# Mixers B and C of a hybrid diffusion block: zero-padded products replaced by pairs of 64-row products

## The chip, the cores and the metric

The kernel runs on one core of one Trainium2 chip. The metric is the device time of one execution in microseconds (us). A change of under 0.2% cannot be told from none on this kernel.

## The reference

One layer of a backbone over 2048 latent tokens of 1024 channels, with 256 context tokens that share its weights. After a norm and one input projection three groups of heads work side by side: A, a gated linear recurrence; B, gated linear attention (6 heads of 64); C, an mLSTM matrix memory (6 heads of 64). All run in both directions. Their outputs are normalised and gated, go through an output projection and then a squared-ReLU MLP. The change lies in the chunked products of B and C (chunks of 64 in the reference, of 128 in the kernel, which is the same sum):

```
B:  scores  = where(causal, q_dec @ k_dec.T, 0)         # per head, direction and chunk
    out     = scores @ v  +  q_dec @ s_prev
C:  w       = (q @ k.T) * exp(log_d - m_row)            # per head; q @ k.T serves both directions
    num     = w @ v  +  e_in * (q @ C_prev)             # second term: the carried product
    C_prev  is updated per chunk by  e_end * k.T @ v
```

Each q @ k.T and q @ C_prev contracts over the 64 channels of one head.

## The kernel before

The program is one in-order list for TensorE (PE): its instructions stand as the code emits them. The other engines' lists are ordered by a scheduler that keeps data dependences. The input projection is cut into small pieces, three matmuls each (lines 365 to 367), and a filler (`fil.run(us)`) drops so many us of them between the products of the mixers, so that PE has work while other engines prepare the next operand.

**Mixer C** (`mix_c`, from line 805) walks 16 chunks of 128 tokens, three pairs of heads each: 48 steps. Two heads lie on the two halves of the partitions. Step i puts on PE, in this order: `scores(i+1)` (line 898: one product of `k3` with `q6`, whose other half is zero for each head, 128 contraction rows, 256 columns); for the first pair of a chunk transposes of the keys (830), for the second the state update `upd_s` (841, weights 64 columns wide); filler; `outputs(i)` (925: four products of 65 columns); `carried(i+1)` (913: two products of 130 columns with the zero-padded `q6`); filler. On VectorE (DVE) line 902 makes the decay weights, 905 multiplies them with the scores, 926 adds the output products to the carried term, 847 updates the state. ScalarE (ACT) takes the exponential (904) and copies the carried product out of PSUM (916).

PSUM has 8 banks: 3 for `pp`, 1 for `tr`, and in mixer C 2 for `qk` (two buffers), 1 for `o2` (carried products and state updates), 1 for `o1` (output products).

**Mixer B's output part** (end of `mix_b`) walks 24 steps (4 groups of 512 tokens, 6 heads). `scores(i+2)` loads q and k (both directions of a head on the two halves of the partitions), copies the two halves of q into a zero-padded tile `bx` (1147 on ACT, 1148 on DVE), makes four products of 256 columns (1155), and takes them from PSUM by an ACT copy and a DVE predicated copy in two halves (1157, 1158), then 1159. `between(i)` follows with filler or pieces of the output projection (1264 to 1266), then `outputs(i)` (1166, 1167). The q tile has 4 buffers, the k tile 3, and the loads are issued in order by SyncE (SP).

An fp32 product stands in the trace as two passes, each a weight load (PEld) and a MATMUL: 8 for the four products at line 1155.

Of the kernel before, what the change touches and what calls it, by code (L numbers as in the profile page):

```python
# [11 lines left out]
F32 = mybir.dt.float32  # L12
# [3 lines left out]
ALU = mybir.AluOpType  # L16
# [4 lines left out]
P = 128  # L21
# [90 lines left out]
def body(ctx: ExitStack, tc: tile.TileContext, I, out, dbg=None, stage=99):  # L112
    nc = tc.nc
# [24 lines left out]
    def spool(stack, name, side="right", bufs=1):  # L138
        return stack.enter_context(tc.tile_pool(name=name, bufs=bufs, side=side, reuse_waits="tile"))

    def psum(stack, name):
        return stack.enter_context(tc.tile_pool(name=name, bufs=1, space=PSUM, reuse_waits="tile"))
# [123 lines left out]
    for k in range(KC):  # L266
        for j in range(4):
            i = 4 * k + j
# [128 lines left out]
    def dgrp(nm, shape_of, groups, dt=F32):  # L397
        return {g: dram.tile(shape_of(GRP[g][1]), dt, name=f"{nm}_{g}") for g in groups}
# [67 lines left out]
    qcD = dgrp("qcD", lambda n: [3, P, n], LATG)  # L466
# [339 lines left out]
    def mix_c():  # L806
        st = ExitStack()
        cp = spool(st, "mxc")
        pm = psum(st, "pmc")

        qz = [cp.tile([P, 6, P], F32, name=f"qz{i}") for i in range(2)]
        for t_ in qz:
            nc.gpsimd.memset(t_, 0.0)
        csD = [dram.tile([P, 3, 65], F32, name=f"csD{c}") for c in range(NCH)]

        def load_kv(c):
            g = 0 if c < 2 else 1 + (c - 2) // 4
            o = c * P - GRP[g][0]
            k3 = cp.tile([P, 3, P], F32, name="k3", bufs=2)
            nc.sync.dma_start(k3, kcD[g][:, :, o:o + P].rearrange("b p t -> p b t"))  # L820
            v3 = cp.tile([P, 6, 65], F32, name="v3", bufs=2)
            nc.gpsimd.memset(v3[:, :, 64:65], 1.0)
            nc.sync.dma_start(v3[:, :, 0:64], vcD[g][o:o + P, :].rearrange("t (h e) -> t h e", e=64))
            return g, o, k3, v3
# [10 lines left out]

        def upd_s(c, d, kb, v3, s_old, s_new):

            u = pm.tile([P, 512], F32, name="o2", bufs=1)
            for h in range(6):
                p, hl = h // 2, h % 2  # L840
                nc.tensor.matmul(u[64 * hl:64 * hl + 64, p * 65:p * 65 + 65], kb[:, h, :], v3[:, h, :])
            for p in range(3):
                up = u[:, p * 65:p * 65 + 65]
                if s_old is None:
                    nc.vector.tensor_copy(s_new[:, p, :], up)
                else:
                    nc.vector.scalar_tensor_tensor(s_new[:, p, :], s_old[:, p, :], abc[:, p, d, c:c + 1], up,
                                                   op0=ALU.mult, op1=ALU.add)
# [4 lines left out]
        for c in [1, 0] + list(range(NCH - 1, 2, -1)) + [None]:  # L853
            if c is not None:
                g, o, k3, v3 = load_kv(c)
# [14 lines left out]
        for c in range(2):  # L870
            g, o, k3, v3 = load_kv(c)
# [8 lines left out]

        def head(c):
            g, o, k3, v3 = load_kv(c)
            q6 = qz[c % 2]
            for hl in range(2):
                hs = slice(64 * hl, 64 * hl + 64)
                nc.sync.dma_start(q6[hs, hl::2, :], qcD[g][:, hs, o:o + P].rearrange("b p t -> p b t"))
            ys = cp.tile([P, 3, P], F32, name="yc", bufs=2)
            cur[c] = (g, o, k3, v3, q6, ys)

        def scores(c, p):  # L890
            if p == 0:
                head(c)
            g, o, k3, v3, q6, ys = cur[c]
            rb = cp.tile([P, 2, 2, P], F32, name="rb", bufs=2)
            for d in range(2):
                nc.sync.dma_start(rb[:, :, d, :], rD[d][g][2 * p:2 * p + 2, o:o + P].unsqueeze(0).to_broadcast([P, 2, P]))
            qk = pm.tile([P, 512], F32, name="qk", bufs=2)
            nc.tensor.matmul(qk[:, 0:256], k3[:, p, :], q6[:, 2 * p:2 * p + 2, :])
            w = cp.tile([P, 2, 2, P], F32, name="wd", bufs=2)
            for hl in range(2):  # L900
                for d in range(2):
                    nc.vector.scalar_tensor_tensor(w[:, hl, d, :], rb[:, hl, d, :], TM[:, c, 0, 2 * p + hl, d:d + 1],
                                                   lm[:, d, :], op0=ALU.add, op1=ALU.min)
            nc.scalar.activation(w, w, AF.Exp)
            nc.vector.tensor_tensor(w, w, qk[:, 0:256].rearrange("p (h l) -> p h l", h=2).unsqueeze(2).to_broadcast([P, 2, 2, P]),
                                    op=ALU.mult)
            return w

        def carried(c, p, states):
            q6 = cur[c][4]  # L910
            o2 = pm.tile([P, 512], F32, name="o2", bufs=1)
            for hl in range(2):
                nc.tensor.matmul(o2[:, hl * 130:hl * 130 + 130], q6[:, 2 * p + hl, :], states[:, p, :, :])
            nm = cp.tile([P, 4, 65], F32, name="nm", bufs=2)
            hd = TM[:, c, :, 2 * p:2 * p + 2, :].rearrange("p q h d -> p q (h d)")
            nc.scalar.copy(nm, o2[:, 0:260].rearrange("p (h e) -> p h e", e=65))
            nc.gpsimd.tensor_tensor(nm, nm, hd[:, 1, :].unsqueeze(2).to_broadcast([P, 4, 65]), op=ALU.mult)
            return nm, hd

        def outputs(c, p, w, nm, hd):  # L920
            g, o, k3, v3, q6, ys = cur[c]
            o1 = pm.tile([P, 512], F32, name="o1", bufs=1)
            for hl in range(2):
                for d in range(2):
                    nc.tensor.matmul(o1[:, (hl * 2 + d) * 65:(hl * 2 + d) * 65 + 65], w[:, hl, d, :], v3[:, 2 * p + hl, :])
            nc.vector.tensor_tensor(nm, nm, o1[:, 0:260].rearrange("p (h e) -> p h e", e=65), op=ALU.add)
            dn = cp.tile([P, 4], F32, name="dn", bufs=2)
            nc.vector.scalar_tensor_tensor(dn, nm[:, :, 64], -1.0, nm[:, :, 64], op0=ALU.mult, op1=ALU.max)
            nc.vector.tensor_tensor(dn, dn, hd[:, 3, :], op=ALU.max)
            nc.vector.reciprocal(dn, dn)  # L930
            yy = cp.tile([P, 4, 64], F32, name="yy", bufs=2)
            nc.gpsimd.tensor_tensor(yy, nm[:, :, 0:64], dn.unsqueeze(2).to_broadcast([P, 4, 64]), op=ALU.mult)
            y4 = yy.rearrange("p (h d) e -> p h d e", d=2)
            nc.gpsimd.tensor_tensor(ys[:, p, :].rearrange("p (h e) -> p h e", h=2), y4[:, :, 0, :], y4[:, :, 1, :], op=ALU.add)
            if p == 2:
                nc.sync.dma_start(yD[g][o:o + P, 640:1024], ys.rearrange("p a b -> p (a b)"))
                cur.pop(c)

        seq = [(c, p) for c in range(2, NCH) for p in range(3)]
        states = {2: s_fw}  # L940
# [5 lines left out]
        for i, (c, p) in enumerate(seq):  # L946
# [11 lines left out]
            w = ws.pop(i)  # L958
# [20 lines left out]
    def mix_b(between):  # L979
# [19 lines left out]
        pm = psum(st, "pmb")  # L999
        bp = spool(st, "mxb")  # L1000
# [4 lines left out]
        sel = bp.tile([P, P], I32, name="sel")  # L1005
# [103 lines left out]
        for i in range(LAST):  # L1109
            if i < len(seq):  # L1110
                hh, g = seq[i]
# [9 lines left out]
            if 0 <= i3:  # L1121
                hh, g = seq[i3]
# [8 lines left out]
            pass  # L1131

        qz = [bp.tile([P, 2, 512], F32, name="bx", bufs=3) for _ in range(3)]
        for t_ in qz:
            nc.gpsimd.memset(t_, 0.0)

        def scores(i, p, g, hl):
            hh = 2 * p + hl  # L1140
            q, k = bt("bk", 4), bt("bq", 3)
            nc.sync.dma_start(q, qdD[hh][g])
            nc.sync.dma_start(k, kdD[hh][g])
            s = bp.tile([P, 4, 64], F32, name="bv", bufs=3)
            nc.gpsimd.dma_start(s, sD[hh][:, 4 * g - 4:4 * g, :])
            z = qz[i % 3]
            nc.scalar.copy(z[0:64, 0, :], q[0:64, :])
            nc.vector.tensor_copy(z[64:128, 1, :], q[64:128, :])
            w = bt("lr" if i % 2 else "bkt")
            wv = w.rearrange("p (c l) -> p c l", l=P)  # L1150
            for jj in (0, 2):
                sc = pm.tile([P, 2, 2, P], F32, name="qk2", bufs=4)
                for j in range(2):
                    js = slice((jj + j) * P, (jj + j + 1) * P)
                    nc.tensor.matmul(sc[:, j, :, :], k[:, js], z[:, :, js])
                wj = wv[:, jj:jj + 2, :]
                nc.scalar.copy(wj, sc[:, :, 0, :])
                nc.vector.copy_predicated(wj, sel.unsqueeze(1).to_broadcast([P, 2, P]), sc[:, :, 1, :])
            nc.vector.tensor_tensor(wv, wv, eye1.unsqueeze(1).to_broadcast([P, 4, P]), op=ALU.mult)
            return q, s, w  # L1160

# [9 lines left out]
        o = v = None  # L1171
        for i in range(-2, len(seq)):
# [5 lines left out]
            p, g, hl = seq[i]  # L1178
            if hl == 0:
# [3 lines left out]
                o = trt()  # L1183
# [561 lines left out]
```

## Time and profile before

| what | value |
|---|---|
| time, median of 3 runs | 2805.06 us (2803.17 to 2809.77) |
| the profiled execution | 2810.26 us, of which its span is 2808.5 us |
| mean granted clock of TensorE | 0.958 |
| PE busy, DVE busy, ACT busy | 2559.5, 1775.4, 1162.4 us |
| mixer C's 48 steps | about 577 to 803 us of the span |
| mixer B's output part | about 1116 to 1281 us of the span |

PE is busy in 91% of the span. A busy row is modelled from the start of the MATMUL to its end, and MATMULs overlap in the pipeline, so the distance between starts tells the pace, not the duration of one.

### The profile page before, as it was taken

To read this page: it belongs to the slowest core of one execution; us is meant where nothing else is said; L and a number is where in the kernel's file an instruction comes from. 1 tells how busy PE (TensorE), PEld (TensorE's weight loads), DVE (VectorE), ACT (ScalarE), POOL (GpSimd) and SP (SyncE) were. 2 spreads that over 40 slices of the span, in tenths; PEclk is the share of its full clock that TensorE was granted. 3 is DMA by queue.
4 is the path that set the end of the run, shared out by engine and by line. 5 is a ranking of instruction groups with operands and counts; after the bars stand their busy time and mean duration, and the time that the engine had idled before them with its cause. 6 is when DMAs were issued, how large, how long until landed. Compare 5 with 4: busy or idle time off the path is not lost. (4 is left out here: it accounts for less than half of the span.)

```text
span 2808.5 us, 36451 instructions
## 1 busy us (share of the span) xinstructions
PE 2559.5 (91%) x12239; PEld 2084.5 (74%) x12239; DVE 1775.4 (63%) x3041; ACT 1162.4 (41%) x2039; POOL 986.9 (35%) x868
## 2 busy tenths in 40 slices
PE   6798889899998888889996999989997999999997
PEld 3576667788887667777775888778885888878876
DVE  7955476156647886646657777766664275565576
ACT  6745421233335656433324444544444333222343
POOL 5724411245444443324444333333431222222211
PEclk7999989999999999889998999999998999999999
DMA  7443355666556665856754776655556576776564
GB/s 221 144 132 109 96 160 161 159 158 161 152 158 171 187 180 168 277 169 207 230 175 127 200 213 200 175 162 156 144 154 203 165 250 196 233 248 211 156 196 150
DMA packets 496455, 499.44 MB, mean 178 GB/s; under 512 B 88578, under 2 KB 371932, under 8 KB 496268
## 3 DMA queue, kind: packets, MB, share of 16 engines
q1 hardware_dynamic: 470316, 469.77, 55.6%
q10 hardware_dynamic: 20480, 15.73, 1.7%
q0 software_dynamic: 5472, 11.60, 1.5%
q8 instruction: 97, 1.59, 0.2%
q14 instruction: 90, 0.74, 0.1%
HBM read 345.27 MB, written 151.72 MB: 177 GB/s over the span
## 5 line engine op out<-in xcount | busy, mean ns | idle before, releaser
L365 PE MATMUL pp<-hTh,whi 128*128 128x512 f32 (+1 forms) x1048 | 435.1, 415 | 15.7 <-DVE evt L505 12.1
L367 PE MATMUL pp<-hTh,wlo 128*128 128x512 f32 (+1 forms) x1048 | 409.2, 390 | 2.2 <-POOL wlo L313 2.0
L366 PE MATMUL pp<-hTl,whi 128*128 128x512 f32 (+1 forms) x1048 | 407.3, 389 | 0.2 <-DVE hTl L452 0.2
L1714 PE MATMUL yps<-bh,ah 128*128 128x512 f32 x896 | 351.9, 393 | 17.5 <-ACT bh L1629 17.1
L1716 PE MATMUL yps<-bh,al 128*128 128x512 f32 x896 | 352.4, 393 | 12.0 <-DVE al L1421 11.2
L1715 PE MATMUL yps<-bl,ah 128*128 128x512 f32 x896 | 351.4, 392 | 0.5 <-DVE bl L1421 0.5
L1421 POOL TENSOR_TENSOR al<-ar,ah 128x1024 fp32r<-128x1024 f32 x56 | 141.8, 2531 | 504.3 <-ACT ah L1643 504.3
L1643 ACT CAST ah<-ar 128x1024 fp32r<-128x1024 f32 x112 | 117.9, 1053 | 359.0 <-PE yps L1715 313.3
L365 PEld LDWEIGHTS pp<-hTh,whi 128*128 128x128 f32 x1048 | 205.7, 196 | 53.4 <-DVE evt L505 14.0
L367 PEld LDWEIGHTS pp<-hTh,wlo 128*128 128x128 f32 x1048 | 204.0, 195 | 45.8 <-POOL wlo L313 3.7
L366 PEld LDWEIGHTS pp<-hTl,whi 128*128 128x128 f32 x1048 | 205.7, 196 | 35.5 <-issue 1.9
L1714 PEld LDWEIGHTS yps<-bh,ah 128*128 128x128 f32 x896 | 170.0, 190 | 53.5 <-ACT bh L1629 17.6
L1716 PEld LDWEIGHTS yps<-bh,al 128*128 128x128 f32 x896 | 169.9, 190 | 50.6 <-DVE al L1421 13.2
L1715 PEld LDWEIGHTS yps<-bl,ah 128*128 128x128 f32 x896 | 170.0, 190 | 36.6 <-DVE bl L1421 1.0
L1424 POOL TENSOR_TENSOR uz<-tz 128x512 f32<-128x512 f32 x32 | 50.3, 1572 | 387.1 <-ACT whi L1455 273.5
L1464 PE MATMUL accy<-th,wlo 128*128 128x512 f32 x384 | 151.2, 394 | 1.3 <-DVE wlo L1421 1.3
L1462 PE MATMUL accy<-th,whi 128*128 128x512 f32 x384 | 150.5, 392 | 1.7 <-DVE tz L1424 1.7
L1463 PE MATMUL accy<-tl,whi 128*128 128x512 f32 x384 | 150.3, 391 | 0.0
L1421 DVE TENSOR_TENSOR wlo<-wab,whi 128x512 fp32r<-128x512 f32 x128 | 117.1, 916 | 42.8 <-ACT whi L1455 42.8
L1421 DVE TENSOR_TENSOR wlo<-ws,whi 128x512 fp32r<-128x512 f32 x96 | 84.4, 879 | 92.0 <-ACT whi L1455 91.8
L1455 ACT CAST whi<-wab 128x512 fp32r<-128x512 f32 x128 | 79.2, 619 | 135.6 <-PE accy L1463 56.4
L1627 DVE TENSOR_TENSOR braw<-braw 128x1024 f32<-128x1024 f32 x56 | 75.0, 1339 | 72.5 <-DMA braw<-in_mlp_w_dram 69.6
(384 smaller groups left out, 5959.0 us busy)
## 6 DMA issues: line engine op xcount, KB each, us to landing
uD<-uz SPq DMA_DIRECT2D x224, 256.0 KB
ar<-uD SPq DMA_DIRECT2D x112, 512.0 KB
braw<-in_mlp_w_dram SPq DMA_DIRECT2D x112, 512.0 KB
wab<-in_mlp_w_dram SPq DMA_DIRECT2D x64, 512.0 KB
maw<-in_ada_w_dram SPq DMA_DIRECT2D x64, 256.0 KB
wraw<-in_w_in_dram SPq DMA_DIRECT2D x54, 256.0 KB
rb<-rD SPq DMA_DIRECT2D x96, 128.0 KB
aw<-in_ada_w_dram SPq DMA_DIRECT2D x32, 256.0 KB
```

The source lines that it names most:

```text
L365: nc.tensor.matmul(acc[:, 0:n], hi, hTh[g][:, k, :], start=k == 0, stop=False)
L366: nc.tensor.matmul(acc[:, 0:n], hi, hTl[g][:, k, :], start=False, stop=False)
L367: nc.tensor.matmul(acc[:, 0:n], lo, hTh[g][:, k, :], start=False, stop=k == KC - 1)
L1421: eng.tensor_tensor(o, a, b, op=ALU.subtract)
L1455: nc.scalar.copy(hi, w)
L1462: nc.tensor.matmul(acc, hi[:, k, :], T2[i][0][:, k, :], start=first and k == 0, stop=False, skip_group_check=True)
L1463: nc.tensor.matmul(acc, hi[:, k, :], T2[i][1][:, k, :], start=False, stop=False, skip_group_check=True)
L1464: nc.tensor.matmul(acc, lo[:, k, :], T2[i][0][:, k, :], start=False, stop=k == 3, skip_group_check=True)
L1643: nc.scalar.copy(hi, r_)
L1714: nc.tensor.matmul(acc, ah[:, p_, :], bh, start=p_ == 0, stop=False)
L1715: nc.tensor.matmul(acc, ah[:, p_, :], bl, start=False, stop=False)
L1716: nc.tensor.matmul(acc, al[:, p_, :], bh, start=False, stop=p_ == 7)
```

## The change

Every zero-padded product becomes a pair of products of 64 contraction rows, one on partitions 0 to 63 and one on 64 to 127, which write to two different PSUM banks. In mixer C the q tile is loaded whole, `qk` becomes one buffer of two banks, and `o1` and `o2` become one tile `oc` of two banks that is allocated once: its columns 0 to 129 hold the carried products, 130 to 259 the output products, 260 to 454 the state update (in the bank of the chunk's parity). In mixer B the copies of q and the padded tiles go, and the scores of the two directions lie in two banks, taken from PSUM by one ACT copy and one predicated copy.

```
-        qz = [cp.tile([P, 6, P], F32, name=f"qz{i}") for i in range(2)]
-        for t_ in qz:
-            nc.gpsimd.memset(t_, 0.0)
+        oc = pm.tile([P, 2, 512], F32, name="oc")
...
-            u = pm.tile([P, 512], F32, name="o2", bufs=1)
+            u = oc[:, c % 2, 260:455]
...
-            q6 = qz[c % 2]
-            for hl in range(2):
-                hs = slice(64 * hl, 64 * hl + 64)
-                nc.sync.dma_start(q6[hs, hl::2, :], qcD[g][:, hs, o:o + P].rearrange("b p t -> p b t"))
+            q6 = cp.tile([P, 3, P], F32, name="q3", bufs=2)
+            nc.sync.dma_start(q6, qcD[g][:, :, o:o + P].rearrange("b p t -> p b t"))
...
-            qk = pm.tile([P, 512], F32, name="qk", bufs=2)
-            nc.tensor.matmul(qk[:, 0:256], k3[:, p, :], q6[:, 2 * p:2 * p + 2, :])
+            qk = pm.tile([P, 2, 512], F32, name="qk")
+            for hl in range(2):
+                hs = slice(64 * hl, 64 * hl + 64)
+                nc.tensor.matmul(qk[:, hl, 0:P], k3[hs, p, :], q6[hs, p, :])
...
-            o2 = pm.tile([P, 512], F32, name="o2", bufs=1)
             for hl in range(2):
-                nc.tensor.matmul(o2[:, hl * 130:hl * 130 + 130], q6[:, 2 * p + hl, :], states[:, p, :, :])
+                hs = slice(64 * hl, 64 * hl + 64)
+                nc.tensor.matmul(oc[:, hl, 0:130], q6[hs, p, :], states[hs, p, :, :])
...
-            o1 = pm.tile([P, 512], F32, name="o1", bufs=1)
             for hl in range(2):
                 for d in range(2):
-                    nc.tensor.matmul(o1[:, (hl * 2 + d) * 65:(hl * 2 + d) * 65 + 65], w[:, hl, d, :], v3[:, 2 * p + hl, :])
-            nc.vector.tensor_tensor(nm, nm, o1[:, 0:260].rearrange("p (h e) -> p h e", e=65), op=ALU.add)
+                    nc.tensor.matmul(oc[:, hl, 130 + d * 65:195 + d * 65], w[:, hl, d, :], v3[:, 2 * p + hl, :])
+            nv = nm.rearrange("p (h d) e -> p h (d e)", d=2)
+            nc.vector.tensor_tensor(nv, nv, oc[:, :, 130:260], op=ALU.add)
...
-            z = qz[i % 3]
-            nc.scalar.copy(z[0:64, 0, :], q[0:64, :])
-            nc.vector.tensor_copy(z[64:128, 1, :], q[64:128, :])
...
+            sc = [pm.tile([P, 4, P], F32, name="qk2", bufs=4) for _ in range(2)]
+            for j in range(4):
+                js = slice(j * P, (j + 1) * P)
+                for d in range(2):
+                    ds = slice(64 * d, 64 * d + 64)
+                    nc.tensor.matmul(sc[d][:, j, :], k[ds, js], q[ds, js])
+            nc.scalar.copy(wv, sc[0])
+            nc.vector.copy_predicated(wv, sel.unsqueeze(1).to_broadcast([P, 4, P]), sc[1])
```

The first place where the order of instructions shows it is PE's list in mixer C, from the output products of one step to the scores of the next but one; the words in brackets are the semaphores that an instruction waits for. Before:

```order
L925 MATMUL o_5729<-v_5660,wd 128x65 [waits DMAHW1_49,DVE_49]
L925 MATMUL o_5729<-v_5660,wd 128x65 x3
L913 MATMUL o_5742<-cs,qz_4475 128x130 [waits Activation_49]
L913 MATMUL o_5742<-cs,qz_4475 128x130
L365 MATMUL pp<-hTh_75,whi 128x512
L366 MATMUL pp<-hTl_76,whi 128x512
L367 MATMUL pp<-hTh_75,wlo 128x512
```

Now, at the same place (the output products are at line 923, the carried ones at 912):

```order
L923 MATMUL oc<-v_5627,wd 128x65 [waits DMAHW5_49,Activation_49]
L923 MATMUL oc<-v_5627,wd 128x65 x3
L912 MATMUL oc<-cs,q_5630 128x130 [waits DVE_49]
L912 MATMUL oc<-cs,q_5630 128x130
L365 MATMUL pp<-hTh_75,whi 128x512
L366 MATMUL pp<-hTl_76,whi 128x512
L367 MATMUL pp<-hTh_75,wlo 128x512
```

The products stand in the same order. The carried products waited for ACT, whose instruction is the copy of the carried term one step earlier (916); now they wait for DVE. In the built program the count that they wait for is the one that DVE reaches with the addition of this same step's output products (line 925 of the changed kernel, 926 before).

On DVE at the same place the list is the same as before, up to names. Before:

```order
L905 TENSOR_TENSOR wd<-wd,qk 128x512 [waits PE_49,Activation_49]
L926 TENSOR_TENSOR nm<-nm,o_5729 128x260 [waits PE_49,Pool_49]
L902 SCALAR_TENSOR_TENSOR wd<-rb,TM,lm 128x128 [waits DMAHW4_49]
L928 SCALAR_TENSOR_TENSOR dn<-nm 128x4 [waits DVE_49]
L902 SCALAR_TENSOR_TENSOR wd<-rb,TM,lm 128x128 [waits DMAHW5_49]
```

Now:

```order
L904 TENSOR_TENSOR wd<-wd,qk 128x512 [waits PE_49,Activation_49]
L925 TENSOR_TENSOR nm<-nm,oc 128x260 [waits PE_49,Pool_49]
L901 SCALAR_TENSOR_TENSOR wd<-rb,TM,lm 128x128 [waits DMAHW7_49]
L927 SCALAR_TENSOR_TENSOR dn<-nm 128x4 [waits DVE_49]
L901 SCALAR_TENSOR_TENSOR wd<-rb,TM,lm 128x128 [waits DMAHW0_49]
```

The addition still follows the multiplication of the next step's weights with their scores, and nothing has come between them.

The third place is PE's list in mixer B's output part, one step's scores. Before:

```order
L1155 MATMUL qk_10971<-bx,bq 128x256 [waits DMAHW3_49,DVE_49]
L1155 MATMUL qk_10971<-bx,bq 128x256
L1155 MATMUL qk_10976<-bx,bq 128x256 [waits DVE_49]
L1155 MATMUL qk_10976<-bx,bq 128x256
L1166 MATMUL tr<-bU,lr 128x64 [waits DVE_49]
```

Now (1148 are the scores, 1158 the first output products):

```order
L1148 MATMUL qk_10878<-bk,bq 128x128 [waits DMAHW7_49,DMAHW3_49,Activation_49]
L1148 MATMUL qk_10879<-bk,bq 128x128 [waits DVE_49]
L1148 MATMUL qk_10878<-bk,bq 128x128
L1148 MATMUL qk_10879<-bk,bq 128x128
L1148 MATMUL qk_10878<-bk,bq 128x128
L1148 MATMUL qk_10879<-bk,bq 128x128
L1148 MATMUL qk_10878<-bk,bq 128x128
L1148 MATMUL qk_10879<-bk,bq 128x128
L1158 MATMUL tr<-bU,lr 128x64 [waits DVE_49]
```

Four products have become eight, whose outputs alternate between two banks. The first waits for the loads of q and k themselves (the two DMA semaphores).

## Rows read from the trace of the kernel before

**Rows 1.** Stretches: us, busy us and instructions by engine, clock, DMA share, GB/s.

```profile
577.00:640.00 63.00, 63.00 (x427) 54.57 (x425) 37.69 (x125) 21.98 (x45) 30.38 (x51) 1.00 0.59 153
640.00:720.00 80.00, 79.59 (x547) 69.46 (x547) 50.76 (x172) 26.93 (x54) 38.16 (x65) 1.00 0.58 156
720.00:803.00 83.00, 82.98 (x548) 72.21 (x548) 53.86 (x177) 30.03 (x59) 42.19 (x69) 1.00 0.56 140
1116.00:1160.00 44.00, 40.83 (x224) 36.17 (x222) 27.77 (x53) 21.59 (x46) 16.51 (x17) 0.92 0.77 233
1160.00:1200.00 40.00, 30.58 (x163) 27.45 (x163) 30.38 (x49) 17.08 (x37) 16.64 (x19) 0.83 0.83 274
1200.00:1258.00 58.00, 48.63 (x255) 42.37 (x255) 26.60 (x51) 17.83 (x38) 13.75 (x17) 0.85 0.53 159
```

**Rows 2.** Timeline, one step of mixer C: start us, us, instruction [idle before <-releaser].

```profile
644.09 1.00 PE L925 MATMUL o<-v,wd 128*128 128x65 f32 x8
...
644.92 0.67 PE L913 MATMUL o<-cs,qz 128*128 128x130 f32 x4
...
645.20 0.43 DVE L926 TENSOR_TENSOR nm<-nm,o 128x260 f32<-128x260 f32 x1 [0.52 <-PE o L925]
...
645.34 0.48 PE L365 MATMUL pp<-hTh,whi 128*128 128x512 f32 x1
...
645.66 0.40 PE L366 MATMUL pp<-hTl,whi 128*128 128x512 f32 x1
```

**Rows 3.** Line 926: durations in ns (min/median/max), and what ended DVE's waits.

```profile
L926 DVE TENSOR_TENSOR nm<-nm,o x48: 417/426/426, 585.7 to 802.0; 128x260 f32<-128x260 f32 x48
...
  PE o L925: 44.3, 37
```

**Rows 4.** Timeline, a place where PE waits for DVE.

```profile
888.74 0.69 DVE L505 TENSOR_TENSOR evt<-evt,pp 128x512 f32<-128x512 f32 x1
...
889.48 0.51 PE L365 MATMUL pp<-hTh,whi 128*128 128x512 f32 x1 [2.68 <-DVE evt L505]
...
889.83 0.40 PE L366 MATMUL pp<-hTl,whi 128*128 128x512 f32 x1
```

**Rows 5.** Timeline of PE around one state update with weights of 64 columns.

```profile
641.54 0.59 PE L898 MATMUL qk<-qz,k 128*128 128x256 f32 x2
642.06 0.57 PE L841 MATMUL o<-v,kb 128*64 128x65 f32 x12
642.56 0.39 PE L365 MATMUL pp<-hTh,whi 128*128 128x256 f32 x1
642.78 0.28 PE L366 MATMUL pp<-hTl,whi 128*128 128x256 f32 x1
642.90 0.28 PE L367 MATMUL pp<-hTh,wlo 128*128 128x256 f32 x1
```

**Rows 6.** Line 841, durations of one pass in ns.

```profile
L841 PE MATMUL o<-v,kb x408: 220/222/272, 519.5 to 782.4; 128*64 128x65 f32 x136
```

**Rows 7.** Timeline of PE, one step of mixer B's output part.

```profile
1179.57 1.98 PE L1155 MATMUL qk<-bx,bq 128*128 128x256 f32 x8 [1.50 <-ACT bx L1147]
1181.39 0.33 PE L1166 MATMUL tr<-bU,bkt 128*128 128x64 f32 x2
```

**Rows 8.** PE's waits, 1100 to 1290 us: us in total, times, longest.

```profile
PE qk L1155 <- ACT bx L1147: 9.6, 6, 2.5
PE qk L1155 <- DVE bx L1148: 8.4, 2, 4.4
```

**Rows 9.** Line 1147: durations in ns, and what ended ACT's waits.

```profile
L1147 ACT COPY bx<-bk x24: 605/617/622, 1086.0 to 1248.7; 64x512 f32<-64x512 f32 x24
...
  DMA bk<-qd: 13.6, 10
```

**Rows 10.** Line 1148, durations in ns.

```profile
L1148 DVE COPY bx<-bk x24: 418/424/3323, 1086.1 to 1249.6; 64x512 f32<-64x512 f32 x24
```

**Rows 11.** The SP queue's waits, 1100 to 1290 us.

```profile
SPq L1142 <- PE tr L1167: 39.5, 20, 7.5
```

More of the change, by code (lines that the diff above doesn't have):

```diff
@@ L904, in scores @@
             nc.scalar.activation(w, w, AF.Exp)
-            nc.vector.tensor_tensor(w, w, qk[:, 0:256].rearrange("p (h l) -> p h l", h=2).unsqueeze(2).to_broadcast([P, 2, 2, P]),
+            nc.vector.tensor_tensor(w, w, qk[:, :, 0:P].unsqueeze(2).to_broadcast([P, 2, 2, P]),
                                     op=ALU.mult)
@@ L910, in carried @@
             q6 = cur[c][4]
-            o2 = pm.tile([P, 512], F32, name="o2", bufs=1)
             for hl in range(2):
-                nc.tensor.matmul(o2[:, hl * 130:hl * 130 + 130], q6[:, 2 * p + hl, :], states[:, p, :, :])
+                hs = slice(64 * hl, 64 * hl + 64)
+                nc.tensor.matmul(oc[:, hl, 0:130], q6[hs, p, :], states[hs, p, :, :])
             nm = cp.tile([P, 4, 65], F32, name="nm", bufs=2)
             hd = TM[:, c, :, 2 * p:2 * p + 2, :].rearrange("p q h d -> p q (h d)")
-            nc.scalar.copy(nm, o2[:, 0:260].rearrange("p (h e) -> p h e", e=65))
+            nc.scalar.copy(nm.rearrange("p (h d) e -> p h (d e)", d=2), oc[:, :, 0:130])
             nc.gpsimd.tensor_tensor(nm, nm, hd[:, 1, :].unsqueeze(2).to_broadcast([P, 4, 65]), op=ALU.mult)
@@ L1131, in mix_b @@
             pass
-        qz = [bp.tile([P, 2, 512], F32, name="bx", bufs=3) for _ in range(3)]
-        for t_ in qz:
-            nc.gpsimd.memset(t_, 0.0)
         def scores(i, p, g, hl):
@@ L1145, in scores @@
             nc.gpsimd.dma_start(s, sD[hh][:, 4 * g - 4:4 * g, :])
-            z = qz[i % 3]
-            nc.scalar.copy(z[0:64, 0, :], q[0:64, :])
-            nc.vector.tensor_copy(z[64:128, 1, :], q[64:128, :])
             w = bt("lr" if i % 2 else "bkt")
             wv = w.rearrange("p (c l) -> p c l", l=P)
[L1151 to L1158, printed above, removed]
+            sc = [pm.tile([P, 4, P], F32, name="qk2", bufs=4) for _ in range(2)]
[6 more added lines that the diff above has]
+            nc.vector.copy_predicated(wv, sel.unsqueeze(1).to_broadcast([P, 4, P]), sc[1])
             nc.vector.tensor_tensor(wv, wv, eye1.unsqueeze(1).to_broadcast([P, 4, P]), op=ALU.mult)
```

## The prediction

> **What bounds the kernel now.** I read the stretches first: they tell which stage has room. In mixer C PE is busy 63.00 of 63, 79.59 of 80 and 82.98 of 83 us at a clock of 1.00 [rows 1]. No engine can be waited for there without PE standing still, so whatever is added to PE's list in these 226 us, work or wait, moves the end by as much, and whatever is taken out is gained. In mixer B's output part PE has gaps (40.83 of 44, 30.58 of 40, 48.63 of 58), the clock is 0.92, 0.83 and 0.85, and the DMA engines are busy 0.77, 0.83 and 0.53 [rows 1]. PE's own waits there are 9.6 us for the ACT copy of q and 8.4 us for the DVE copy [rows 8]. The loads of q in turn wait for the output products of an earlier step, 39.5 us in 20 times [rows 11], so that part is a loop of load, copy, scores and outputs, with PE full in some steps and short of data in others.
>
> **The change, part by part. The new wait.** PE's order of products in mixer C stays, but the carried products now wait for DVE's addition of the same step's output products, since both use the tile `oc`. The timeline prices it. The output products' last pass is followed by the carried ones at 644.92; the addition starts at 645.20 and takes 0.43, to 645.63 [rows 2]. It took 417 to 426 ns in all 48 steps, and in 37 of them DVE stood waiting for these products [rows 3], so it can start no earlier, and DVE's list puts nothing new ahead of it. PE resumes 0.05 after DVE's end: 888.74 and 0.69 make 889.43, and PE starts at 889.48 [rows 4]. So the carried products start at 645.68 and not at 644.92: 0.76 us in which PE does nothing. Queued behind them on PE are the filler, the scores of the next but one step, and all that follows; ACT's copy of the carried term waits for them too, but has the filler's time to spare.
>
> **Pairs and their switch.** The carried products were four passes in 0.42 us (644.92 to 645.34), 0.105 each, and the eight passes of the output products, though of half the columns, also come 0.104 apart (644.09 to 644.92) [rows 2]: the weight load sets this pace. No pair on two halves of the contraction rows stands in the trace. The nearest row is the state update, pairs on two halves of the weight columns: twelve passes of which the last ends after 0.57 us, and one takes 0.22 [rows 5, 6], so twelve starts lie within 0.35 us, 0.029 apart, two at a time. I take the same for the row halves, since this is the only pair that the trace has: two pairs at 0.105. The other end is no overlap at all, four passes at 0.105.
>
> The same rows price the change from whole-array products to halves and back. Eight passes of 256 columns take 1.82 us (1179.57 to 1181.39), about 0.1 of it the late first [rows 7], so 0.215 each; the two from 641.54 are through at 641.97, and the state update starts at 642.06: 0.09 lost going in. Its last pass starts at 642.41 and streams for 0.06; the next product starts at 642.56, 0.09 later, and is followed after 0.22 where the pace is 0.12: 0.10 more [rows 5]. So 0.09 in and 0.19 out. I take these for the row halves as well; the other bound is zero, products that go side by side without a break.
>
> The Trainium skill, in TensorEngine Tiling (Array Packing), Key Properties, says that a change of the tiling mode, unlike one of the tile, drains TensorE. It speaks against a change that switches mode for two products at a time. The rows around the state update agree with it, at 0.28 us for in and out; for row halves no row shows it. By the rule the sum is the one taken here, without it that of the first rival.
>
> Carried, per step: from 645.68, 0.10 for a first weight load that no product covers (the same 0.10), two pairs 0.21, out 0.09: the filler starts at 646.08, not 645.34. Its next pass is late in both cases (645.66 after 645.34, 0.32 [rows 2]), so 0.74 stays. 47 steps have it (the first carried products stand ahead of the loop): +34.8 us.
>
> Scores of mixer C: before, two passes at 0.215, 0.43. Now in 0.09, first load 0.10, two pairs 0.21, out 0.19: 0.59. In 33 steps +0.16, 5.3 us; in the 15 with a state update right behind, which had to switch anyway, I count nothing. One buffer for `qk` instead of two adds no wait: the multiplication that frees it stands ahead of the addition in DVE's list, and PE has waited for that addition by then. Were this order lost, up to 0.69 a step would show. The output products of those 15 steps now wait for the third state addition on DVE; the 1.5 us of filler between 642.56 and 644.09 hides it; uncovered, it would be 0.3 a step, 4.5 us.
>
> Scores of mixer B: eight passes, 1.73 us, become eight pairs at 0.105 with 0.38 of switching and first load, 1.22: -0.51, in 24 steps -12.2 us. Without overlap sixteen passes and 0.38 make 2.06: +0.33, +7.9 us.
>
> The copies of q go. Each of the six waits for ACT falls by at least its 0.62 [rows 9] and the 0.05 of the signal: 4.0 of 9.6 us. The two waits for DVE (8.4 us) stood behind a copy that once took 3.32 instead of 0.42 us [rows 10]; I take 6. That makes -10, to which -12 for the scores adds. But ACT itself waited 13.6 us for these loads [rows 9], and where a load is late PE now waits for it. Of 22 I take 18. The bounds are -31 (all of the 10, no switching: 24 times 0.89 for the scores) and +8 (pairs do not overlap and loads take over all waits).
>
> Edits at nothing: the removed memsets on POOL, fewer issues on SP, and the wider copies out of PSUM, all on engines that are busy half of the time or less in mixer C's and B's stretches, save DVE in one [rows 1].
>
> Sum: 34.8 + 5.3 - 18 = +22. The profiled execution took 2810.3 (span 2808.5), which becomes 2832; the median of the runs is 5.2 lower, so 2827.
>
> **Rivals.** First, faster: row halves need no switch. Then the carried products cost 645.68 + 0.10 + 0.21 = 645.99, 0.65 late, less the 0.09 by which the next filler pass need no longer be late: 0.56 times 47, 26 us. The scores in mixer C gain 0.22 times 48, 10 us; mixer B gains 25 to 31. Sum -9 to -15: 2790 to 2796. For it: the 0.09 and 0.19 were seen at column halves alone. Against it: they come at each of the state updates, and a half is a half. It decides from a switch of about 0.1 us on; above that the sum is no longer negative.
>
> Second, the pairs do not overlap, and the change doesn't do what it says. Carried 0.74 + 0.21, 47 times, 45; scores in mixer C 0.38 a step, 33 times, and 0.21, 15 times, 16; mixer B -10 and +8. Sum +59: 2864. For it: two weight loads of 128 columns have never been seen at once here. Against it: twelve starts in 0.35 us. The skill, TensorE: Matmul & The Clock Gate, Part 3, has products on different row groups run at the same time; no row here shows it, and by it this rival falls away.
>
> Third, mixer B gains little, because the loads bound it (0.83 of DMA time [rows 1]): +40 - 3, 2842.
>
> Fourth, the clock: in mixer B's part, where PE has gaps, it stands at 0.83 to 0.92 [rows 1]. Were it 0.92 in mixer C too, now that PE stands still in each step, 8% of 266 us, 21, would come on top of the 22: 2848. Against it: gaps of 0.8 us, where mixer B's are up to 4.4 [rows 8].
>
> **How the numbers follow.** Chances: the forecast 0.51 (its own range 2817 to 2838), no switch 0.13, no overlap 0.17, no gain in mixer B 0.13, the clock 0.04, 0.02 for what I do not see. The range from 2795 to 2860 leaves out about half of the first rival and most of the second. 0.2% of the median is 5.6 us, less than which the measurement cannot tell from none. Faster: most of the first rival, 0.11. The same: its rest and the lower edge of the forecast, 0.08. Slower: 0.81.
>
> **What would show it.** In the changed profile: PE busy some 0.86 of mixer C and not all of it; in each step a gap of about 0.8 us ahead of the carried products, ended by DVE's addition, some 36 us in total; the 48 steps about 40 us longer than 226; pairs of starts under 0.02 us apart, at 64 rows; the product after a pair late by about 0.2; no wait of scores in mixer B for ACT or DVE, but some for loads. I am wrong if the carried products do not wait (then mixer C would end within 10 us of where it did), or if mixer B's part gains over 35 us.

## The result and the profile after

The changed kernel takes 2846.9 us, the median of 4 runs (2842.5 to 2849.0), the kernel before 2805.6 (4 runs, 2803.2 to 2809.8). The ratio of the means is 1.0143, with a 95% interval of 1.0123 to 1.0163; that is +41 us where +22 was forecast. The profiled execution took 2849.0, its span 2847.2 (2808.5 before). Following the same PE instructions through both traces puts the 38.7 us between the spans in these places:

| stretch | before, us | after, us | difference |
|---|---|---|---|
| up to the first scores of mixer C | 578.7 | 584.1 | +5.4 |
| mixer C's 48 steps, first scores to last output products | 222.1 | 263.4 | +41.3 |
| to the first scores of mixer B's output part | 315.9 | 313.3 | -2.6 |
| mixer B's output part, first scores to last output product | 163.9 | 157.8 | -6.1 |
| the rest | 1527.8 | 1528.7 | +0.9 |

The first row is mostly scatter: in the twelve profiles of the experiments mixer C's first scores come between 574.1 and 581.4 us, at 581.4 and 576.8 in the two that have the change in mixer C. (584.1 is still 2.7 above them all; whether the change costs something there is not shown.) So mixer C cost what was forecast (+40.1), and in this one trace mixer B gave 6 where 18 were forecast. The stretches after, in the columns of [rows 1]:

```profile
584.00:640.00 56.00, 50.13 (x350) 39.78 (x345) 26.96 (x99) 16.27 (x32) 22.05 (x38) 1.00 0.49 134
640.00:720.00 80.00, 70.84 (x485) 55.85 (x484) 38.33 (x147) 25.17 (x49) 32.84 (x56) 0.98 0.49 130
720.00:800.00 80.00, 71.25 (x488) 56.07 (x486) 36.86 (x143) 23.54 (x47) 32.46 (x58) 1.00 0.47 128
...
1160.00:1188.00 28.00, 24.32 (x204) 20.76 (x204) 18.73 (x28) 12.16 (x21) 10.52 (x11) 0.99 0.77 244
1188.00:1273.00 85.00, 85.00 (x492) 79.87 (x490) 38.52 (x59) 22.68 (x40) 29.12 (x35) 0.50 0.74 236
```

In mixer C, PE is busy 0.89 of the time and not all of it, at a clock of 0.98 to 1.00. The last row is the surprise: 85 us of mixer B in which PE never stands still, at 1.2 GHz throughout. Before, no stretch of mixer B's part at that clock lasted over 10.2 us.

One step of mixer C, to be set beside [rows 2]:

```profile
660.18 1.00 PE L923 MATMUL oc<-v,wd 128*128 128x65 f32 x8
...
661.28 0.43 DVE L925 TENSOR_TENSOR nm<-nm,oc 128x260 f32<-128x260 f32 x1 [1.68 <-PE oc L923]
...
661.76 0.49 PE L912 MATMUL oc<-cs,q 64*128 64x130 f32 x4 [0.59 <-DVE nm L925]
...
662.19 0.50 PE L365 MATMUL pp<-hTh,whi 128*128 128x512 f32 x1
...
662.53 0.40 PE L366 MATMUL pp<-hTl,whi 128*128 128x512 f32 x1
```

The addition ends at 661.71 and the carried products start 0.05 later, 1.58 after the first output product; before, it was 0.83. All 47 of them wait so:

```profile
PE oc L912 <- DVE nm L925: 28.0, 47, 0.9
PE oc L923 <- DVE cs L846: 0.9, 1, 0.9
```

The 28.0 us are less than the loss, since the profile counts the last pass as busy to its modelled end. The starts are the safer measure. The second row is the wait for the third state addition, counted at nothing in the prediction: 0.9 us once.

The scores' pairs on the two halves of the rows, half a step later:

```profile
663.45 0.40 PE L367 MATMUL pp<-hTh,wlo 128*128 128x512 f32 x1
663.78 0.49 PE L897 MATMUL qk<-q,k 64*128 64x128 f32 x4
664.20 0.50 PE L365 MATMUL pp<-hTh,whi 128*128 128x512 f32 x1
664.54 0.39 PE L366 MATMUL pp<-hTl,whi 128*128 128x512 f32 x1
```

The pair starts 0.33 after a pass that else is followed after 0.23: 0.10 to go in. In the single records the four starts are 663.778 and 663.785, 663.992 and 663.998: 0.007 apart in a pair, the second pair 0.21 after the first (0.10 of it the late first load). The filler comes 0.20 later and its next pass 0.34 after it: 0.20 to come out. That is the price read from the column halves, 0.09 and 0.19 [rows 5]. The Trainium skill's rule in TensorEngine Tiling (Array Packing), Key Properties, that a change of mode drains TensorE, agrees with these rows, for row halves too.

Mixer B's part, PE at the place where its clock falls (1187.2 us), and where it rises again (1275.9):

```profile
1180.97 1.16 PE L1148 MATMUL qk<-bk,bq 64*128 64x128 f32 x16
1182.06 0.43 PE L1158 MATMUL tr<-bU,lr 128*128 128x64 f32 x2
...
1183.67 0.39 PE L1159 MATMUL tr<-bv,bk 128*128 128x64 f32 x2
1187.45 2.08 PE L1148 MATMUL qk<-bk,bq 64*128 64x128 f32 x16 [3.40 <-issue]
1189.46 0.69 PE L1158 MATMUL tr<-bU,bkt 128*128 128x64 f32 x2
...
1271.65 2.08 PE L1148 MATMUL qk<-bk,bq 64*128 64x128 f32 x16
1273.66 1.97 PE L1239 MATMUL pp<-ident,yt 128*128 128x128 f32 x8
1276.39 0.50 PE L1256 MATMUL pp<-woh,yh 128*128 128x512 f32 x1 [0.76 <-ACT yh L1242]
```

At 2.4 GHz the scores take 1.09 us to the next product (1.73 by the forecast's reckoning before, 1.22 forecast), and a step of scores and outputs 3.0 us. After one wait of 3.40 us they run at 1.2 GHz: 2.01 for the scores, 5.61 from step to step, 16 steps long, until the output projection's products come (its transposes of 128 columns at 1273.66, its products of 512 columns from 1276.39). Before, 17 steps of the same part, from 1136.88 to 1232.14, took 5.60 each on average, with PE waiting in between. PE's waits for copies, 18.0 us before [rows 8], are gone:

```profile
PE qk L1148 <- issue: 3.7, 2, 3.4
PE pp L1258 <- POOL yl L1243: 1.1, 2, 0.6
PE pp L1256 <- ACT yh L1242: 0.8, 1, 0.8
```

### The profile page after: what moved, and what is told of

Same layout as the page of the kernel before. It is cut to its first block, busy times and chain, and to the rows that moved or that the text cites. A ratio compares the mean times of both kernels' runs of the same rounds, so it can differ in the third digit from the quotient of the medians.

```text
span 2847.2 us, 36874 instructions
## 1 busy us (share of the span) xinstructions
PE 2583.8 (91%) x12527; PEld 2088.9 (73%) x12527; DVE 1740.8 (61%) x2993; ACT 1149.9 (40%) x1991; POOL 980.9 (34%) x863
```

## The experiments

Each result gives the median in us, then the ratio of the mean times to the kernel before and its 95% interval. The theory: mixer C's loss is the wait for DVE alone, and mixer B's gain is eaten by the clock. The rivals: the pairs and their switches make the loss, and the loads limit mixer B.

**Each mixer alone.** `c_only` has the diff's edits in mixer C, `b_only` those in mixer B.

> Mixer C with the change, mixer B as before. The theory (the trace of after set against before): all of mixer C's loss, +41 us, stays, and perhaps the 3 us that the loop over the backward states lost ahead of it; 2846 to 2852, and the 48 steps take 264 us. The theory's split of the 41: 0.75 us more from the first output product to the first carried one in 47 steps (35), 0.11 more per score pair, 0.06 more ahead of it. Rival: part of the 41 comes from a change of clock or of loads that mixer B's part shares; then it is under +35.

> Mixer B with the change, mixer C as before. By the prediction's term -18: 2787. By the alignment of the two traces -8 to -9: 2796. The clock theory: the part has a long stretch at a granted clock of 0.50, with the scores at about 2.05 us and the outputs at 3.2 us a step, and 5.6 us a step; without it the gain would be the forecast 18 or more. The rival, loads: the steps are set by the DMA engines, 5 us and more apart at either clock, and PE stands waiting between them.

`c_only`: 2851.1, 1.0162 (1.0140 to 1.0185), mixer C 262.1 us, +40.0. `b_only`: 2803.5, 0.9987 (0.9972 to 1.0001): some 3 us, which cannot be told from none, and less than the 8 to 9 that the two traces set side by side had said. Its middle is two rows (columns as above):

```profile
1139.80:1179.60 39.80, 39.78 (x228) 37.41 (x230) 21.01 (x29) 11.61 (x20) 15.30 (x19) 0.50 0.78 251
1179.60:1224.00 44.40, 44.40 (x256) 41.67 (x253) 17.75 (x31) 11.05 (x20) 13.55 (x17) 0.50 0.75 232
```

The same 1.2 GHz and 5.61 us a step as in the profile of after, here after a wait of 2.2 us, and PE full. Mixer B's part compared, with the next two kernels (PE idle is length less busy time):

| kernel | scores of mixer B | length, us | PE idle, us | mean granted clock |
|---|---|---|---|---|
| before | whole array | 163.9 | 22.6 | 0.89 |
| c_only | whole array | 160.2 | 22.2 | 0.91 |
| wait_only | whole array | 156.0 | 18.4 | 0.91 |
| no_wait | whole array | 159.1 | 19.3 | 0.90 |
| after | pairs | 157.8 | 5.5 | 0.72 |
| b_only | pairs | 160.0 | 4.7 | 0.70 |

The length scatters by 8 us among the four kernels with nothing changed in it, so one trace's 6 us gain was no measure. Idle time was traded for a slower clock.

**The wait alone.** Whole-array products as before, but one tile:

```
-            o2 = pm.tile([P, 512], F32, name="o2", bufs=1)
-                nc.tensor.matmul(o2[:, hl * 130:hl * 130 + 130], q6[:, 2 * p + hl, :], ...)
+                nc.tensor.matmul(oc[:, hl, 0:130], q6[:, 2 * p + hl, :], ...)
```

and so the output products and the state update (`oc[:, c % 2, 260:455]`).

> The kernel before with one thing of the change alone: the output products, the carried products and the state update of mixer C share the tile of two banks, all products whole-array and zero-padded as before. The theory (the wait is the loss): 0.75 us more a step between the first output product and the first carried one, 47 steps, +35: 2840, 2836 to 2843. Rival (the pairs and their switch make the loss, the wait would be hidden): under 2815.

2844.6, 1.0145 (1.0126 to 1.0164), 1.6 above the expected range; mixer C 260.6, +38.5. The same gap stands in the trace (timeline of PE, one step):

```profile
666.05 1.00 PE L924 MATMUL oc<-v,wd 128*128 128x65 f32 x8
...
667.65 0.71 PE L913 MATMUL oc<-cs,qz 128*128 128x130 f32 x4 [0.59 <-DVE nm L926]
...
668.11 0.48 PE L365 MATMUL pp<-hTh,whi 128*128 128x512 f32 x1
```

From the first output product to the first carried one it is 1.602 on average, as in after (1.602), and 0.857 before: 0.745 in 47 steps, 35.0 us. Some 2.3 more come from the product after the idle time. The pairs themselves are the difference from `c_only`: +1.5 us. In `oc` the two uses share the tile and also its two banks; which of the two makes the order was not taken apart.

**The wait hidden.** Mixer C's pairs, with the carried products behind the six filler passes that followed them (two lines swapped); mixer B as before.

> Mixer C with the change, but the carried products stand behind the six filler passes (1.4 us) that followed them, so DVE's addition is through when they come; mixer B as before. The wait theory: of the 41 us in mixer C 35 go; a state update now waits for ACT's copy of the carried products, up to 0.5 us in 16 chunks, and carried products and scores stand side by side, which spares a switch: 2805 to 2818. Rival (pairs and switches cost more than they seem): above 2825.

2821.7, 1.0069 (1.0048 to 1.0091); mixer C 235.2, so 27 of the 40 us are back, and the expected range was missed by 4. What is late next, by PE's waits:

```profile
PE oc L840 <- POOL yc L933: 8.9, 11, 0.9
PE oc L912 <- DVE nm L925: 3.1, 6, 0.6
```

Five steps have no filler there and keep the old wait. The state update now waits too, 8.9 us in 11 chunks under this name and 10.3 in 15 in all. POOL is not what it waits for:

```profile
704.38 0.45 POOL L933 TENSOR_TENSOR yc<-yy 128x128 f32<-128x128 f32 x1
704.41 0.36 ACT L915 COPY nm<-oc 128x260 f32<-128x260 f32 x1
...
704.91 0.47 PE L840 MATMUL oc<-v,kb 128*64 128x65 f32 x9 [0.85 <-POOL yc L933]
```

In all 15 chunks the update starts 0.14 after the end of ACT's copy of the carried products out of `oc`, while POOL's instruction ended 0.02 to 3.6 before it, and the keys that POOL scales for the update 0.8 to 3.9. It is the expected wait for ACT, a second one within the same tile, and longer than the 0.5 expected. With it the account closes: 10.3 and 3.1 are about the 13 us that are left.

**The clock or the loads.** `b_only` with useless work for PE: one or two products of 512 columns a step from the fifth step on, overwritten by the scores (here one).

```
+            if i >= 4:
+                nc.tensor.matmul(sc[0], ident, ident.unsqueeze(1).to_broadcast([P, 4, P]))
```

> Mixer B alone with the change, and from the fifth step on one product of 128 columns of weights by 512 columns, of the identity, into the score tile ahead of the scores; its output is overwritten. It adds 0.86 us of PE a step at 2.4 GHz (two passes of 512 columns, 0.84 ns a column as in the whole-array scores). The clock theory: the stretch at a granted clock of 0.50 (some 90 us in mixer B's change alone) shortens, a step takes 2.9 + 0.9 us of PE, the loads become the bound at about 4.1 us (0.74 of 5.6): 16 steps by 1.5 us less, 2780, 2775 to 2792. The rival (the loads set the 5.6 us, the clock is only a consequence): 2803 or above, and 0.9 to 1.7 us a step more where the clock stays low, up to 2830.

> The same with two such products a step, 1.72 us at 2.4 GHz. The clock theory: more surely at 2.4 GHz, a step takes 2.9 + 1.7 = 4.6 us of PE and not 5.6: 2787, 2780 to 2797. The rival: 2803 to 2860.

`b_warm`: 2798.1, 0.9969 (0.9953 to 0.9984): more work and no more time, though not the 2780 expected. It is faster than the kernel before; against `b_only` the intervals overlap. Where the clock holds, a step takes 4.4 us (scores at 1160.62 and, six steps on, 1187.00):

```profile
1160.60:1187.00 26.40, 23.98 (x206) 18.39 (x205) 21.41 (x32) 10.79 (x20) 14.64 (x17) 1.00 0.96 312
```

There PE has gaps again and the DMA engines are busy 0.96: with the clock up, the loads are the limit, 1.2 us below the slow clock's 5.61. Then a load came 3.2 us late, and four steps ran at 1.2 GHz after all. `b_warm2`: clock 0.97 in the part, but 1.72 us a step cost as much as they won: 2805.6, 0.9997 (0.9983 to 1.0011), above its range. The time at a granted clock of 0.50 in mixer B's part fell with the added work: 95.6 us in one stretch in `b_only`, 6.8 and 23.9 in `b_warm`, 3.4 and 6.8 in `b_warm2`. So both explanations are true, one behind the other.

**Fewer loads** was to be `b_woc0` (`WOC` = 0, the projection's weights converted after mixer B).

> Mixer B alone with the change, and none of the output projection's weights loaded or converted until mixer B is through: some 256 KB a step less to load between the steps. Read by the distance of the scores, not by its time, since the projection starts later. The clock theory: where the granted clock is 0.50 a step takes the same 5.6 us as in b_only (5.60 to 5.62), whatever the loads. If no load is late any more, the clock stays at 1.00 and a step takes 3 to 4 us, and mixer B's part ends 30 us earlier. The rival (loads set the 5.6 us): steps of 4 to 4.8 us at a granted clock that may still be 0.50.

It is inconclusive for the loads: only PE's order moved, the weights' loads went out as early as before (1118.6 to 1177.7 us), and the DMA share stayed at 0.75 (0.76 in `b_only`). Its single run took 2813.6 us against 2801.5 of the kernel before. It does show 18 steps in a row at 1.2 GHz, all but the first two 5.61 us apart, until the projection's products come.

**Do the halves run at once?** `b_halves`: the loop over the halves outside that over the four blocks.

> Mixer B alone with the change, but the eight score products in another order: the four of the upper half of the rows first, then the four of the lower half, so that no two neighbours are a pair. The theory (two products run side by side only as neighbours on different halves): a burst of 16 passes at 2.4 GHz takes 16 times 0.105 and the switch, 1.9 to 2.1 us, where pairs take 1.15; at 1.2 GHz 3.6 to 4. Rival (no overlap is needed, the pace is set elsewhere): 1.15 as before. As time: 0 to +20 us, by where PE is late.

```profile
1127.55 1.71 PE L1149 MATMUL qk<-bk,bq 64*128 64x128 f32 x16
1129.19 0.43 PE L1159 MATMUL tr<-bU,lr 128*128 128x64 f32 x2
```

1.71 us for the 16 passes against 1.16 as pairs (3.1 against 2.08 at 1.2 GHz). Neighbours on different halves do overlap; the rival is dead. Its steps at 1.2 GHz are 6.63 us apart instead of 5.61, longer by what the scores take more: at that clock PE sets the step, and the loads do not. (The single run took 2817.4 us.) 1.71 is less than expected: in the single records the second four start at 1128.10, while passes of the first four still start up to 1128.43.

**A better version.** If steps of scores and outputs alone let the clock fall, wide products should start earlier: `b_only` with `WLAG, WREADY, WOC = 2, 7, 2` instead of 1 at the end (`b_woc2`), and 3 (`b_woc3`), the same in the kernel before (`before_woc2`), and `b_woc2` with one overwritten product in steps 4 to 13 (`woc2_warm`).

> Mixer B alone with the change, and the weights of the output projection converted two tiles a step instead of one, so that the wide products of that projection (24 passes of 512 columns) start in about the 13th of the 24 steps and not the 21st. The clock theory: the steps with nothing but scores and outputs go from 16 to 9 and the stretch at 0.50 with them, 90 to about 45 us: 10 to 25 us less than mixer B's change alone, 2780 to 2795. The rival (the loads are the bound, and the weights now come twice as densely): 2800 to 2820.

> The kernel before with the weights of the output projection converted two tiles a step, mixer B's scores whole-array with copies as before: the control for b_woc2 (2788, -17). If the earlier start of the wide products alone makes that gain: 2785 to 2793. If it needs the change in mixer B, whose steps alone leave PE no idle time and a long stretch at a granted clock of 0.50: within 5 us of 2806.

> b_woc2 with one product of 512 columns (0.86 us at 2.4 GHz, its output overwritten) ahead of the scores in the ten steps that have no wide products. The clock theory: those steps go from 5.6 us towards the 4.3 that b_warm showed, less what the loads take: 2 to 10 us less than b_woc2, 2778 to 2786. The rival (the loads, now with twice the weights, are the bound in these steps): 2788 or a few us above.

> Mixer B alone with the change, weights of the output projection converted three tiles a step: the wide products start two steps earlier than in b_woc2. If the clock is what is left: another 2 to 5 us less, 2783 to 2786. If the loads are: 2788 to 2798.

| kernel | median, us | ratio of means to before | interval |
|---|---|---|---|
| before_woc2 | 2799.2 | 0.9973 | 0.9962 to 0.9984 |
| b_woc2 | 2788.3 | 0.9939 | 0.9916 to 0.9961 |
| b_woc3 | 2783.6 | 0.9932 | 0.9908 to 0.9956 |
| woc2_warm | 2785.0 | 0.9922 | 0.9897 to 0.9947 |

All are faster than the kernel before and the changed one; the last three cannot be told apart. The overwritten product of `woc2_warm` shortened the long stretch at 1.2 GHz from 51.2 to 20.5 us without a gain in time that could be told from none. The control lies between its two expectations: the earlier start alone gives 7 us, and mixer B's pairs, worth at most some 3 us alone, give 11 on top of it (the two intervals just do not touch).

## Why the forecast came out as it did

The time, 2846.9, lies in the stated range (2795 to 2860) but outside the forecast's own 2817 to 2838. It came to stand beside the third and fourth rivals (2842 and 2848), neither by the mechanism that the runs showed. The term of mixer C was right. That the whole stayed in the range although mixer B's term failed is luck: the upper end had been drawn for pairs that do not overlap, and they do.

- **The new wait** was right in mechanism and size: 0.76 forecast, 0.745 a step measured, and almost nothing net for the pairs and switch behind it (0.77 from the first carried product to the second filler pass in the rows above, 0.74 before [rows 2]). `wait_only` shows the wait by itself.
- **The switch**, 0.09 in and 0.19 out, taken from the column halves: 0.10 and 0.20. The scores of mixer C, +5.3 forecast, are +3.9 by the starts of the passes around them. The no-switch rival falls by this. So the forecast's sum for mixer C stands: +40.1, measured +41.3 and, alone, +40.0.
- **The pairs overlap**, as assumed: 1.09 us against 1.22 forecast in mixer B; the second rival falls.
- **The step that failed** is "Of 22 I take 18". Its two parts came true, the waits for the copies went and the scores became shorter, but the sum reckoned the new passes at the pace of 2.4 GHz and took no account of what the clock would do; [rows 1] had it at 0.83 to 0.92. Mixer B's gain was some 3 us, not told from none, and not 18: PE ran 88.7 us at 1.2 GHz instead. The third rival had its amount (3) by the wrong cause: in `b_warm` loads hold a step to 4.4 us, the clock holds it to 5.61, and 16 steps by 1.2 us are 19, an estimate of what the clock cost and about what is missing. The fourth rival had the right cause in the wrong mixer: it set the clock's fall in mixer C, where 0.98 to 1.00 stayed granted through gaps of 0.6 us, but for one short stretch (678.6 to 682.0 us) behind the longest wait (0.94).
- "No wait of scores in mixer B for ACT or DVE" held; for the 3.7 us that are left the profile names no releaser, so "some for loads" is not shown in after (it is in `b_warm`, 5.7 us). PE busy 0.89 instead of 0.86 in mixer C is the modelled end of a pass.
- One reading of [rows 1] was wrong: DVE is busy over half of the time in five of the six stretches (0.60 to 0.76), not in one. It did not bear on the result: the change took work off DVE in both parts (141 to 126 us in mixer C, 96 to 80 in mixer B's).

## What to carry to other kernels

Two uses that share one tile (here with its banks) order their users: look at which engine must have read the first use before the second may write, and price that engine's whole latency, above all where PE is full. On a stage where PE has idle time, work taken off PE is not time: ask what clock the engine will be granted with less work, and what is late next. Here it paid to start the wide products of the next stage earlier, among the short, narrow ones. Measure a part by several runs, since one trace's part scattered by 8 us here.

## What was not expected of the hardware

- With 64-row scores and 64-column outputs, PE stayed at a granted clock of 0.50 for 88.7 us, and for 95.6, 102.4 and 116.1 in `b_only`, `b_halves` and `b_woc0`, while it was busy almost without a break; a busy PE is no sign of a full clock. It fell there after a single wait of 2.0 to 3.6 us and rose once the output projection ran: during its transposes or right behind them in two of the four, after 5 and 7 us of its products of 512 columns in the others. With whole-array scores, in five kernels, no stretch lasted over 10.2 us, though waits of 1.7 to 4.4 us stand there too. Which property of the products keeps the clock down was not taken apart; that they run as pairs is not needed, since `b_halves` has the same. The Trainium skill, TensorE: Matmul & The Clock Gate, HAM oscillation, tells of a loop that waits for a transfer in every tile and is throttled each time; here the low clock outlasted a single wait by 16 steps.
- Adding 0.86 us of work to 20 of the 24 steps cost no time (2798.1 us against 2803.5 without it).
- Row halves overlap even when the partner comes four products later, though less (1.71 against 1.16 us).
